# A decoder layer on one core: the recurrence's preparation in steps between projection pieces, in a written TensorE order

## The chip, the cores and the metric

One core of one Trainium2 chip runs the whole layer in one launch. The metric is the device time of an execution in microseconds; of several runs the median is given. The core has TensorE (PE; its weight loads are listed apart as PEld), VectorE (DVE), ScalarE (ACT), GpSimd (POOL) and SyncE (SP, which here only issues DMAs). Matmul results land in eight PSUM banks of 128 x 512 fp32; everything else lies in SBUF.

## The reference, cut to what matters

One layer on x of 1024 tokens by 1024 channels: a row norm, one wide projection, three branches, gates, an output projection and a convolutional FFN.

```
h = rms_norm(x, norm1_g)
proj = h @ w_in
p_rwkv, p_sb, q_mem, gate_logits = split(proj)
y_a = rwkv7_branch(p_rwkv)           # delta-rule recurrence, 8 heads x 64
y_b = stick_breaking_branch(p_sb)    # causal attention, 8 heads x 64
y_m = memory_branch(q_mem, mem)      # cross attention into 256 tokens
merged = sum_n sigmoid(gates[n]) * (ys[n] @ w_branch[n])
x = x + merged @ w_out
x = x + conv_ffn(rms_norm(x), ...)
```

In the recurrence r, k and v are mixed with the token before (token shift); a decay, a rate a and a gate g come from small low-rank products; per step S = S * w + (S @ -kk) (kk * a) + v k, y = S r, with kk the normalised k. The kernel computes it in chunks of 64 tokens.

## The kernel before

The channels lie on the partitions. Each fp32 product of a projection is made of three products of split values (hi x hi, hi x lo, lo x hi: `mm3`, line 83), so one projection of 128 channels is 8 k-blocks of six matmuls into two PSUM banks of the tag "mm". Its weights are loaded by SyncE (`load_w`, line 74), rounded by ScalarE (line 80) and the rest taken by GpSimd (line 81); two buffers each. Of the eight banks four have the tag "mm" and four the tag "g" (small products and transposes).

The stages in order:

- `startup` (line 169) loads and splits x, sums the squares of its rows (line 194), runs the first three projections k by k, and only then makes the row norm: eight products with a column of ones, a power on GpSimd (line 167), eight ScalarE copies that spread the result (line 218), transposes, and `rbc`, the norm as a full tile. All evictions of projections need `rbc` (`shifted`, lines 236 to 240).
- For each of four pairs of heads p, `rwkv_prep` (line 283) turns k, r and v into the operands of the recurrence: low-rank products and sigmoids, the sum of squares per head, a scan of the decay (line 334), exponentials, the spread of the head norm (`expand_heads`, line 246), then in two halves VectorE's chain of lines 349 to 353 and the Gram products, masked on VectorE (line 368) and written to DRAM; `turned` products of k by the decay (line 356 on GpSimd, transposes, line 383 on ScalarE). Meanwhile `rwkv_proj` runs the next pair's three projections, and after the last pair `sb_v` the value projection of the attention. `weave` (line 1503) takes some steps of one generator and then some of another; here 0.3 projection per step of the preparation.
- At this stage the order on all engines, TensorE's too, is the planner's: it sorts instructions by priority (`weave` raises that of the preparation) and by its own estimate of when operands are ready. From the attention on `self.pin` is set: matmuls and transposes then keep the order of the program (`pinned`, line 107), while the other engines' orders remain the planner's.
- `sb_attn` (line 674) is the stick-breaking attention: 64 units of head and block; `front` scores and sigmoids, a backwards scan and a multiply on VectorE (lines 698, 699), `mid` transposes, `back` the product with v. Between its steps a pump (`pumped`) takes pieces from a list of items: key and query projections (`sb_qk`), gates (`gate_item`, line 594), the memory branch's projections, later the branch products. `need(name)` pumps until a mark is set.
- `inverse` (line 388) solves the 128 triangular 64 x 64 systems of the recurrence on VectorE: 62 columns, each a product into `it` (line 395) and an addition into `inst` (line 397), on a matrix that GpSimd's queue loads from DRAM (line 386). The pump takes three of its steps per five pieces. Its results go out on GpSimd's queue (line 404) and are read by the recurrence, `stage2`, after the memory attention.
- A gate's banks are read by VectorE, which multiplies by `rbc` (line 603), followed by ScalarE's sigmoid (line 604) and a store.

The rest (branches, output projection, FFN) is not touched.

Of the kernel before, what the change touches and what calls it, by code (L numbers as in the profile page):

```python
# [14 lines left out]
AF = mybir.ActivationFunctionType  # L15
# [34 lines left out]
class Trunk:  # L50
# [118 lines left out]
    def startup(self):  # L169
# [33 lines left out]
        for k in range(8):  # L203
            ks = slice(k * 128, (k + 1) * 128)
            for w, pp in zip(ws, pps):
                self.mm3(pp, [a[:, ks] for a in w], self.xin(k), k == 0, k == 7)
        pst = self.ps("g")
        for j in range(8):
            self.mmul(pst[:, j : j + 1], sqs[-1][:, j * 128 : (j + 1) * 128], self.ones[:, 0:1], start=True, stop=True)
# [6 lines left out]
        ex = self.t4("at")  # L216
        for j in range(8):
            nc.scalar.activation(ex[:, j * 128 : (j + 1) * 128], self.ones, AF.Copy, scale=self.rsc[:, j : j + 1])
        for h in range(2):
            pt = self.ps("g")  # L220
            for j in range(4):
                self.transpose(pt[:, j * 128 : (j + 1) * 128], ex[:, (h * 4 + j) * 128 : (h * 4 + j + 1) * 128])
            nc.scalar.activation(self.rbc[:, h * 512 : (h + 1) * 512], pt, AF.Copy)
        self.wa = self.shifted(12, "A", pps[0])
        nc.scalar.activation(self.wa[0:64], self.wa[0:64], AF.Tanh)
        self.sg = self.shifted(13, "A", pps[1])
        nc.scalar.activation(self.sg, self.sg, AF.Sigmoid)
        return self.shifted(4, "at", pps[2])
# [48 lines left out]
    def rwkv_proj(self, p, out):  # L277
        for i in range(len(out), 3):
            out.append(self.shifted((4, 0, 8)[i] + p, tag="at"))
            yield  # L280

    def rwkv_prep(self, p, krv):
        nc = self.nc
        k, r, v = krv
# [3 lines left out]
        a, g = self.t4("qk"), self.t4("qk")  # L288
# [4 lines left out]
        for hs in halves:  # L293
            pgh = self.ps("g")
            self.mmul(pgh, lora[:, 512 + p * 128 : 512 + (p + 1) * 128], self.sg[:, hs], start=True, stop=True)
            nc.scalar.activation(g[:, hs], pgh, AF.Copy)
# [3 lines left out]
        yield  # L300
        su, P = self.t4("qk"), self.t4("qk", n=1025)
# [4 lines left out]
        nc.scalar.activation(P[:, :1024], k, AF.Square, scale=self.par("k_k", p))  # L306
# [5 lines left out]
        yield  # L312
# [8 lines left out]
        for cc in range(2):  # L321
            nc.scalar.dma_start(self.vd[p // 2, :, :, p % 2 * 2 + cc].rearrange("g s i -> s g i"), vt[cc * 64 : cc * 64 + 64].rearrange("s (g i) -> s g i", g=NG))
# [8 lines left out]
        nc.scalar.dma_start(self.ggd[p, 0], g)  # L331
        yield
        cc = Q = su
        nc.vector.tensor_tensor_scan(cc, self.seg, su, 0.0, ALU.mult, ALU.add)
        nc.scalar.activation(P[:, 1:1025], cc, AF.Exp, scale=-EXPM, bias=self.offs[:, 0:1])
        pc = self.pc[p]
        nc.scalar.activation(pc, cc.rearrange("p (c s) -> p c s", c=NC)[:, :, 63], AF.Exp, scale=-EXPM)
        nc.scalar.activation(Q, cc, AF.Exp, scale=EXPM, bias=self.offs[:, 1:2])
        nc.vector.memset(P[:, 0:1], 0.0)
        bc = self.bcast_heads(self.expand_heads(inv, "qk"))  # L340
        kk, b = k, a
        for h, hs in enumerate(halves):
            nc.vector.scalar_tensor_tensor(kk[:, hs], k[:, hs], self.par("k_k", p), bc[h], ALU.mult, ALU.mult)
        nc.vector.tensor_tensor(b, kk, a, ALU.mult)
        yield
        for h, hs in enumerate(halves):
            bk, ra = self.t4("qk"), self.t4("qk")
            bk4, ra4 = (x.rearrange("p (c u s) -> p c u s", c=8, u=2) for x in (bk, ra))
            nc.vector.tensor_tensor(bk4[:, :, 0], self.c8(b[:, hs]), self.c8(Q[:, hs]), ALU.mult)
            nc.vector.tensor_tensor(bk4[:, :, 1], self.c8(kp[:, hs]), self.c8(Q[:, hs]), ALU.mult)  # L350
            nc.vector.tensor_tensor(ra4[:, :, 0], self.c8(r[:, hs]), self.c8(P[:, 1 + h * 512 : 1 + (h + 1) * 512]), ALU.mult)
            nc.vector.scalar_tensor_tensor(ra4[:, :, 1], self.c8(P[:, hs]), -1.0, self.c8(kk[:, hs]), ALU.mult, ALU.mult)
            nc.vector.tensor_scalar(ra4[:, :, 1, 0], self.c8(kk[:, hs])[:, :, 0], -math.exp(OFF), None, ALU.mult)
            self.spill(p, h, 0, ra, nc.sync)
            bp = self.t4("qk")
            nc.gpsimd.tensor_tensor(
                self.c8(bp), self.c8(bk), pc[:, h * 8 : h * 8 + 8].unsqueeze(2).to_broadcast([128, 8, 128]), ALU.mult)
            for f in range(2):
                mt = self.t4("qk")
                mt4 = mt.rearrange("p (c h t) -> p c h t", c=4, h=2)  # L360
                pm = [self.ps("g"), self.ps("g")]
                for c in range(4):
                    o = (f * 4 + c) * 128
                    for h2 in range(2):
                        q = slice(h2 * 64, h2 * 64 + 64)
                        self.mmul(pm[h2][:, c * 128 : (c + 1) * 128], bk[q, o : o + 128], ra[q, o : o + 128], start=True, stop=True)
                for h2 in range(2):
                    nc.vector.tensor_tensor(
                        mt4[:, :, h2], pm[h2].rearrange("p (c t) -> p c t", c=4),
                        self.mm_mask.unsqueeze(1).to_broadcast([128, 4, 128]), ALU.mult)  # L370
                g0 = h * 4 + f * 2
                nc.sync.dma_start(
                    self.scr[p, g0 : g0 + 2, :, 512:1024].rearrange("g q c -> q g c"), mt.rearrange("q (g c) -> q g c", g=2))
                for h2 in range(2):
                    i0 = p * 32 + h2 * 16 + h * 8 + f * 4
                    nc.sync.dma_start(self.mad[i0 : i0 + 4].rearrange("c s t -> s c t"), mt4[0:64, :, h2, 64:128])
                yield
            bt = self.t4("qk")
            for f in range(2):
                pt = self.ps("g")  # L380
                for c in range(4):
                    self.transpose(pt[:, c * 128 : (c + 1) * 128], bp[:, (f * 4 + c) * 128 : (f * 4 + c + 1) * 128])
                nc.scalar.activation(bt[:, f * 512 : (f + 1) * 512], pt, AF.Copy)
            self.spill(p, h, 256, bt, nc.scalar)
            yield
        nc.gpsimd.dma_start(self.inst[p * 32 : p * 32 + 32], self.mad[p * 32 : p * 32 + 32])

    def inverse(self):
        nc = self.nc
        X = self.inst  # L390
        for s in range(1, 63):
            n = 63 - s
# [1272 lines left out]
```

## Time and profile before

| what | value |
|---|---|
| three runs | 2019.86, 2024.20, 2024.33 us, median 2024.2 |
| profiled execution | 2021.44 us, span from first to last instruction 2019.6 us |
| busy | TensorE 95%, weight loads 77%, VectorE 60%, ScalarE 43%, GpSimd 39% |
| mean granted TensorE clock | 0.978 |
| HBM traffic | 175.83 MB read, 77.33 MB written |

The profile is of one execution. An instruction of the trace has its line, engine, operation and tiles (written out<-in); "idle before" is the time in which its engine did nothing ahead of it, and the name behind the arrow is what released it. A helper's line stands for all its callers, so matmuls carry line 112 and transposes line 105. Matmuls overlap in the pipeline: their rate is read from the distance of their starts. The granted clock is 1 at the full rate; it is given as a mean over a stretch.

### The profile page before, as it was taken

What the parts mean: (1) busy time and instruction counts of PE and PEld (TensorE: products, weight loads), DVE (VectorE), ACT (ScalarE), POOL (GpSimd) and SP (SyncE); (2) the same over time, 40 slices, a digit from 0 to 9 for tenths busy, and PEclk for the clock granted to TensorE, in tenths of its full rate; (3) what the DMA queues carried; (4) which work ended last, traced back from release to release, by engine and by line L of the source; (5) the groups of instructions that cost most, each with busy time, mean ns of one, the idle gap of its engine ahead of it and who ended that gap; (6) DMA issues with size and microseconds to landing.
All of it is one profiled execution on the core that took longest, in us unless ns stands there. A gap on an engine that the chain in (4) does not pass through costs nothing. (4 is left out here: it accounts for less than half of the span.)

```text
span 2019.6 us, 26436 instructions
## 1 busy us (share of the span) xinstructions
PE 1912.1 (95%) x9940; PEld 1546.2 (77%) x9940; DVE 1212.5 (60%) x1783; ACT 874.5 (43%) x1537; POOL 795.1 (39%) x444
## 2 busy tenths in 40 slices
PE   7999989787999999998999989998999999999989
PEld 6676667676888898777777867876888888878877
DVE  4555658899756632433444268247776776786483
ACT  4444322444656653541333323344444454454433
POOL 2222233312323243111132254157767677645453
PEclk9999989888999999999999999999999999999999
DMA  4144552111122332176643354222222232377474
GB/s 186 53 140 152 167 167 84 42 37 35 48 61 58 92 100 76 48 251 195 217 144 128 147 198 170 100 107 78 100 100 96 100 118 78 115 247 276 137 240 164
DMA packets 110735, 254.92 MB, mean 126 GB/s; under 512 B 19472, under 2 KB 32016, under 8 KB 110480
## 3 DMA queue, kind: packets, MB, share of 16 engines
q1 hardware_dynamic: 78736, 190.54, 28.1%
q10 hardware_dynamic: 28096, 50.08, 7.0%
q0 software_dynamic: 3776, 12.62, 2.1%
q8 instruction: 78, 1.28, 0.3%
q14 instruction: 49, 0.40, 0.1%
HBM read 175.83 MB, written 77.33 MB: 125 GB/s over the span
## 5 line engine op out<-in xcount | busy, mean ns | idle before, releaser
L81 POOL TENSOR_TENSOR wl<-wr,wh 128x1024 fp32r<-128x1024 f32 x77 | 197.6, 2567 | 534.5 <-ACT wh L80 508.1
L112 PE MATMUL mm<-xhi,wh 128*128 128x512 f32 x784 | 271.0, 424 | 20.4 <-DVE w L603 10.7
L112 PE MATMUL mm<-xlo,wh 128*128 128x512 f32 x784 | 252.1, 401 | 0.9 <-DVE xlo L181 0.9
L112 PE MATMUL mm<-xhi,wl 128*128 128x512 f32 x784 | 252.4, 401 | 0.0
L80 ACT ACTIVATE wh<-wr 128x1024 fp32r<-128x1024 f32 x77 | 81.7, 1061 | 233.9 <-PE mm L112 204.9
L112 PEld LDWEIGHTS mm<-xlo,wh 128*128 128x128 f32 x784 | 149.9, 191 | 39.9 <-issue 3.0
L112 PEld LDWEIGHTS mm<-xhi,wl 128*128 128x128 f32 x784 | 148.9, 190 | 36.9 <-issue 1.5
L112 PEld LDWEIGHTS mm<-xhi,wh 128*128 128x128 f32 x784 | 138.9, 194 | 48.9 <-DVE w L603 11.5
L698 DVE TENSOR_TENSOR_SCAN at<-at,at 128x128 f32<-128x128 f32 (+3 forms) x64 | 90.6, 1416 | 62.6 <-ACT at L697 57.2
L112 PE MATMUL mm<-dw,da 128*128 128x512 f32 x528 | 120.7, 389 | 1.8 <-DVE da L1419 1.8
L112 PE MATMUL mm<-BT,l 128*128 128x512 f32 x504 | 119.3, 392 | 0.0
L112 PE MATMUL mm<-BT,wh 128*128 128x512 f32 x352 | 111.6, 398 | 6.9 <-DVE u L1237 6.3
L1420 POOL TENSOR_TENSOR dw<-draw,dw 128x512 fp32r<-128x512 f32 x55 | 84.5, 1540 | 85.3 <-ACT dw L1418 83.9
L112 PEld LDWEIGHTS mm<-dw,da 128*128 128x128 f32 x528 | 99.0, 188 | 22.8 <-DVE da L1419 2.2
L112 PE MATMUL mm<-B,wh 128*128 128x512 f32 x352 | 110.5, 395 | 1.7 <-ACT p L1279 1.7
L112 PEld LDWEIGHTS mm<-BT,l 128*128 128x128 f32 x504 | 94.6, 188 | 21.4
L167 POOL TENSOR_TENSOR hf<-rs,half 128x16 f32<-128x16 f32 (+1 forms) x17 | 52.6, 3094 | 123.1 <-DVE rs L166 112.2
L1417 ACT ACTIVATE da<-draw 128x512 fp32r<-128x512 f32 x77 | 48.6, 632 | 120.5 <-PE g L112 48.2
L112 PE MATMUL g<-dw,da 128*128 128x512 f32 x396 | 93.6, 398 | 5.7 <-POOL dw L1420 4.3
L1419 DVE TENSOR_TENSOR da<-draw,da 128x512 fp32r<-128x512 f32 x77 | 60.9, 798 | 54.9 <-ACT da L1417 54.9
L112 PEld LDWEIGHTS g<-dw,da 128*128 128x128 f32 x396 | 76.2, 193 | 22.6 <-POOL dw L1420 4.8
L112 PE MATMUL mm<-at,A 128*128 128x128 f32 (+1 forms) x608 | 91.2, 295 | 1.1 <-DVE qk L863 1.1
(314 smaller groups left out, 4249.3 us busy)
## 6 DMA issues: line engine op xcount, KB each, us to landing
wr<-in_w_in_dram SPq DMA_DIRECT2D x50, 512.0 KB, 3.6
draw<-actd SPq DMA_DIRECT2D x77, 256.0 KB, 3.2
at<-scr SPq DMA_DIRECT2D x32, 512.0 KB, 5.6
draw<-in_w_down_dram SPq DMA_DIRECT2D x55, 256.0 KB, 4.1
scr<-qk SPq DMA_DIRECT2D x24, 512.0 KB, 3.3
wr<-in_w_up_dram SPq DMA_DIRECT2D x22, 512.0 KB, 3.4
actd<-gall ACTq DMA_DIRECT2D x44, 256.0 KB, 3.0
rw<-in_w_up_dram SPq DMA_DIRECT2D x20, 512.0 KB, 3.5
```

Source lines behind the costliest of these rows:

```text
L80: self.nc.scalar.activation(hi, raw, AF.Copy)
L81: self.nc.gpsimd.tensor_tensor(lo, raw, hi.bitcast(F32), ALU.subtract)
L112: self.pinned(self.nc.tensor.matmul(*a, **k))
L167: nc.gpsimd.tensor_tensor(out, t[:, :n], self.half[:, :n], ALU.pow)
L698: nc.vector.tensor_tensor_scan(sn[:, :W][:, ::-1], sn[:, :W][:, ::-1], sp[:, :W], 1.0, ALU.mult, ALU.bypass)
L1417: nc.scalar.activation(A[:, 0], a, AF.Copy)
L1419: nc.vector.tensor_tensor(A[:, 1], a, A[:, 0].bitcast(F32), ALU.subtract)
L1420: nc.gpsimd.tensor_tensor(Wt[:, 1], w, Wt[:, 0].bitcast(F32), ALU.subtract)
```

## The change

- The row norm is a function of its own (`row_norm`, `row_spread`) called inside the first projections' loop, after k = 4 and after k = 6.
- `shift_item` makes a projection of r, k or v an item of the pump's list: one piece of six matmuls per step. `sb_v` becomes eight items of four pieces. Marks say when k and v of a pair are evicted (`settle`).
- `rwkv_prep` is cut into 25 steps (31 for the first pair) and rearranged: decay and scan early, the chain of lines 349 to 353 as `chain(h)`, Gram products as four separate pieces `gram(h, f)`, each a set number of steps behind the chain. Some tiles move to other buffers (`mt` and `bt` from "qk" to "at", `bp` and `ex` to "it").
- `self.pin` is set before the preparation, so TensorE's order is the program's from there on.
- The inverse takes 8 steps per ten pieces after the last preparation and 5 per ten from the attention on; what is left is drained before the branch items. Its VectorE steps, and the attention's scan and multiply (now `weigh`, half a unit later), keep the order of the program.
- A gate's banks are copied by ScalarE; VectorE then multiplies the SBUF copy.

```diff
             for w, pp in zip(ws, pps):
                 self.mm3(pp, [a[:, ks] for a in w], self.xin(k), k == 0, k == 7)
+            if k == 4:
+                self.row_norm(sqs[-1])
+            elif k == 6:
+                self.row_spread()
...
+    def shift_item(self, ti, out, name):
+        w = self.split_w(self.I["w_in"][ti])
+        yield
+        pp = [self.ps("mm"), self.ps("mm")]
+        for k in range(8):
+            ks = slice(k * 128, (k + 1) * 128)
+            self.mm3(pp, [a[:, ks] for a in w], self.xin(k), k == 0, k == 7)
+            if k == 3:
+                self.settle()
+            if k < 7:
+                yield
+        out.append(self.shifted(ti, "at", pp))
+        self.fresh.append(name)
+        yield
...
     def inverse(self):
...
-            nc.vector.tensor_tensor(tv, X[:, 0:s, s : s + 1]...
+            self.pinned(nc.vector.tensor_tensor(tv, X[:, 0:s, s : s + 1]...
...
     def gate_item, fin:
             for h in range(2):
-                hs = slice(h * 512, (h + 1) * 512)
-                nc.vector.tensor_tensor(g[:, hs], pp[h], self.rbc[:, hs], ALU.mult)
+                nc.scalar.activation(g[:, h * 512 : (h + 1) * 512], pp[h], AF.Copy)
+            nc.vector.tensor_tensor(g, g, self.rbc, ALU.mult)
             nc.scalar.activation(g, g, AF.Sigmoid)
...
+        def weigh(u):
+            W = (units[u][3] + 1) * 128
+            sn, sp = st[u]
+            self.pinned(nc.vector.tensor_tensor_scan(sn[:, :W][:, ::-1], ...))
+            self.pinned(nc.vector.tensor_tensor(sp[:, : W - 1], sp[:, : W - 1], sn[:, 1:W], ALU.mult))
...
             if 2 <= u < len(units) + 2:
                 mid(u - 2)
+            if u < len(units):
+                weigh(u)
             yield
...
-        drain(self.rwkv_proj(0, krv[0]))
-        for p in range(4):
-            f = self.rwkv_proj(p + 1, krv[p + 1]) if p < 3 else self.sb_v()
-            self.weave(self.rwkv_prep(p, krv[p]), f, 0.3)
-            drain(f)
+        self.pin = True
+        marks, self.fresh = {"k0"}, []
+        self.marks = marks
+        items = [self.shift_item(i + p, krv[p], f"{n}{p}") for p in range(4) for n, i in (("k", 4), ("r", 0), ("v", 8)) if (p, n) != (0, "k")]
+        items += self.sb_v()
+        inv = self.inverse()
...
-        items += [ld1, gate(), mark("y1"), *br1, ld2, gate(), *br2]
+        items += [lambda: drain(inv), ld1, gate(), mark("y1"), *br1, ld2, gate(), *br2]
...
-        inv = self.inverse()
+        pace = [0]
 
         def pumped():
-            for i, _ in enumerate(self.stream(items)):
-                for _ in range((i * 3 + 3) // 5 - i * 3 // 5):
+            due = 0
+            for _ in self.stream(items):
+                due += pace[0]
+                while due >= 10:
+                    due -= 10
                     next(inv, None)
                 yield
...
-        self.pin = True
+        for p in range(4):
+            self.weave(self.rwkv_prep(p, krv[p], need), pump, 1.0)
+        pace[0] = 8
+        need("sb0")
+        pace[0] = 5
         self.weave(self.sb_attn(qk, need), pump, 1.03, 0)
         need("kv")
-        drain(inv)
         self.weave(self.mem_attn(mq, need), pump, 1.6, 0)
```

The steps of the new `rwkv_prep`, with the number of pieces behind each (for p = 0 six pieces go ahead):

```
a = sigmoid(low-rank), square of k, kp            2
su = sigmoid(low-rank), scan                      2
head sums, norm, g, exponentials, spread ex       3
(needs v) rk, transposes of v, store              2
transposes of ex, kk, b; chain(0); decayed(0)     2
bonus products, stores of bonus and g             3
gram(0,0); chain(1)                               1
gram(0,1)                                         2
turned(0), decayed(1)                             3
gram(1,0)                                         1
gram(1,1)                                         3
turned(1), load of the inverse's matrix           1
```

## The prediction from the page and the trace of before

> **What bounds the kernel now.** I read the page first. TensorE is busy in nearly all of the span; the rest is what can be won.
>
> ```profile
> span 2019.6 us, 26436 instructions
> PE 1912.1 (95%) x9940; PEld 1546.2 (77%) x9940; DVE 1212.5 (60%) x1783; ACT 874.5 (43%) x1537; POOL 795.1 (39%) x444
> ```
>
> Next I cut the span by stage in the view of windows. Columns: stretch, length, then busy us and count of TensorE, weight loads, VectorE, ScalarE, GpSimd; then the granted TensorE clock, DMA share, GB/s. The rows are startup, row norm, preparation of the recurrence with its projections, the rest of those projections, the first attention inputs, early attention, later attention, everything after.
>
> ```profile
> 0.00:46.30 46.30, 38.15 (x160) 30.56 (x160) 22.89 (x23) 22.41 (x22) 11.30 (x9) 1.00 0.47 181
> 46.30:58.50 12.20, 8.37 (x24) 6.01 (x24) 5.92 (x12) 7.23 (x14) 2.73 (x2) 0.58 0.23 83
> 58.50:310.00 251.50, 231.54 (x1171) 174.59 (x1170) 139.58 (x166) 94.77 (x113) 73.11 (x32) 0.97 0.46 141
> 310.00:350.50 40.50, 40.50 (x185) 33.05 (x184) 38.15 (x40) 11.15 (x13) 13.91 (x5) 1.00 0.23 75
> 350.50:386.00 35.50, 22.34 (x100) 18.32 (x99) 27.51 (x33) 10.73 (x12) 10.17 (x3) 0.81 0.08 31
> 386.00:515.00 129.00, 110.28 (x609) 91.72 (x609) 120.58 (x133) 64.30 (x115) 26.59 (x10) 0.92 0.12 38
> 515.00:740.00 225.00, 224.99 (x1365) 192.10 (x1364) 134.76 (x144) 144.19 (x258) 67.22 (x41) 0.99 0.23 68
> 740.00:2019.60 1279.60, 1235.94 (x6339) 999.89 (x6337) 723.11 (x1236) 519.75 (x993) 590.04 (x344) 0.99 0.42 145
> ```
>
> The edits lie in the stages before 740. TensorE idles there 3.8 us in the row norm, 20.0 in the preparation, 13.2 and 18.7 at the start of attention; nothing between 515 and 740. In the same four rows the clock is low as well, so gaps cost twice. VectorE explains the shape: 120.6 of 129 us busy in early attention, 134.8 of 225 later, because the inverse, whose steps were spread over all of attention in the program, ran early.
>
> The waits of TensorE in the first 600 us (engine and what it did, releaser, us in total, times, longest) name the causes:
>
> ```profile
> PE g L112 <- DVE qk L353: 17.7, 8, 3.7
> PE g L105 <- DVE w L246: 13.2, 1, 13.2
> PE mm L112 <- DVE w L603: 10.7, 2, 8.9
> ...
> PE g L105 <- DVE at L699: 4.9, 3, 2.4
> PE g L105 <- ACT at L218: 3.1, 1, 3.1
> PE mm L112 <- ACT w L649: 1.7, 1, 1.7
> ...
> PE g L105 <- DVE hn L557: 1.4, 1, 1.4
> ```
>
> L353 is the last operand before the Gram products of the preparation; L246 spreads the head norm; L603 is VectorE taking a gate out of its banks; L699 weighs the attention; L218 belongs to the row norm.
>
> **Startup.** The row norm moves from behind the projections to the places after their fifth and seventh k. These are rows of the timeline (start, us, engine, line, operation):
>
> ```profile
> 28.82 1.21 DVE L194 TENSOR_TENSOR qk<-qk,qk 128x1024 f32<-128x1024 f32 x1
> 32.01 0.63 PE L112 MATMUL mm<-xhi,wh 128*128 128x512 f32 x2
> 40.38 0.63 PE L112 MATMUL mm<-xhi,wh 128*128 128x512 f32 x2
> 44.57 1.84 PE L112 MATMUL g<-kon,qk 128*128 128x1 f32 x16
> 49.52 2.52 PE L105 MATMUL g<-kon,at 128*128 128x128 f32 x8 [3.10 <-ACT at L218]
> 52.77 0.80 PE L112 MATMUL mm<-xhi,wh 128*128 128x512 f32 x1 [0.73 <-DVE w L236]
> 55.50 1.05 PE L112 MATMUL mm<-xhi,wh 128*128 128x512 f32 x2
> 56.35 1.05 PE L112 MATMUL mm<-xlo,wh 128*128 128x512 f32 x2
> 58.65 0.40 PE L112 MATMUL mm<-xlo,wh 128*128 128x512 f32 x1
> 77.09 0.63 PE L112 MATMUL mm<-xhi,wh 128*128 128x512 f32 x2
> 78.49 0.63 PE L112 MATMUL mm<-xhi,wh 128*128 128x512 f32 x2
> ```
>
> The last sum of squares is ready at 30.0, before the fifth k ends at 32.0; the chain from the sums to the transposes takes 49.5 - 44.6 = 5.0 us, and 8.4 lie between the two new places. So both waits of this chain (3.83) go. The matmuls themselves stay, at the full rate. After the gap a pair of matmuls takes 0.85 us (55.50 to 56.35), at the full rate 1.40 / 3 = 0.47 (77.09 to 78.49 is three pairs): from 52.77 to 58.65 that loses 5.88 x (1 - 0.47 / 0.85) = 2.6. The gain lies between 3.8, the idle alone, and 8.9, with all of the clock loss 0.42 x 12.2 = 5.1. I take 7: both waits, the 2.6 and a little of the slow transposes.
>
> **Preparation.** The same products, projections and DMAs are issued, but TensorE's order is now written: 11 projections and 8 value items give 120 pieces of six matmuls (1.40 us, above), and a preparation is cut into 25 steps with a piece after each. What can be won is all idle and clock of that row: 20.0 + 0.03 x 251.5 = 27.5. What is late next is VectorE's chain again, now with a fixed cover:
>
> ```profile
> 90.87 1.88 PE L112 MATMUL g<-qk,kon 128*128 128x512 f32 x4
> 93.40 1.39 DVE L343 SCALAR_TENSOR_TENSOR at<-at,params,g 128x512 f32<-128x512 f32 x2
> 99.57 1.75 DVE L353 TENSOR_SCALAR qk<-at 128x8 f32<-128x8 f32 x1
> 101.37 2.06 PE L112 MATMUL g<-qk,qk 64*128 64x128 f32 x32 [1.22 <-DVE qk L353]
> 112.36 3.29 PE L112 MATMUL g<-qk,qk 64*128 64x128 f32 x32 [2.51 <-DVE qk L353]
> 114.03 1.29 DVE L240 SCALAR_TENSOR_TENSOR at<-w,omm,w 128x1024 f32<-128x1024 f32 x1 [1.21 <-ACT w L238]
> ```
>
> From the first product with the spread norm (93.40) to the end of L353 (101.32) are 7.9 us. In the new order five pieces (7.0) and the bonus products (1.88) stand between the spread and the first Gram piece: 8.9. That is 1.0 to spare. If a projection's eviction falls in between (two multiplies and L240, some 2.6 us), the operand is 1.6 late. Counting steps, a projection ends inside this stretch for the first three preparations and not for the fourth. The second half has six pieces and a Gram piece, 9.4, against a chain of similar length and the mask multiplies. So I leave three to six waits of 1.6, about 7, and 2 for the clock behind them: 9 of the 27.5 stay, between 0 and 27.5. Gain 18.5.
>
> The clock needs a choice here. After the wait of 1.22 us the Gram products took 2.06, after one of 2.51 they took 3.29, so 2.51 us was enough for slow matmuls. The Trainium skill, "TensorE: Matmul & The Clock Gate", section "What's actually happening", says that the half rate comes after an idle window of about 3.4 us; by that rule my short waits would cost no clock and the forecast would be 2 us lower. The trace decides against it.
>
> Buffers moved from one tag to another are no longer waited for, by my count of live tiles; a spill or weight load that comes late has a projection's whole length of cover (eight pieces, 11 us).
>
> **The inverse and early attention.** The inverse starts after the last preparation, and its first step waits on VectorE for its matrix from DRAM, as today:
>
> ```profile
> 311.01 0.23 DVE L395 TENSOR_TENSOR it<-inst 128x62 f32<-128x62 f32 x1 [17.50 <-DMA inst<-mad]
> ```
>
> Behind it on VectorE stands the first attention head's norm, which TensorE needs after 7 + 8 + 8 pieces, 32 us: the 17.5 stay hidden; uncovered they would cost up to that. Then 0.8 steps per piece, from attention on 0.5, all pinned between the weighings. VectorE's work up to 740 stays (120.6 + 134.8 us from 386 on), over 354 - 32 = 322 us: 79% busy rather than 93% and then 60%. So the 13.2 at L246 and the 10.7 at L603 go: the norm no longer queues behind inverse steps, and gates leave through ScalarE. Idle of both rows: 31.9. The clock there: 0.19 x 35.5 + 0.08 x 129 = 17.1, but much of it falls into the gaps themselves, where it costs nothing. I take 7, 2.6 after each of three long waits as at startup. Of the 39 the waits behind the weighing and the head norm (4.9 + 1.4) and a little clock stay: 7. Gain 32, between 0 and 49.
>
> The inverse ends later, some 20 pieces (28 us) before the memory attention is through; its results then go out from GpSimd's queue before the recurrence loads them:
>
> ```profile
> L404 POOL DMA_DIRECT2D td<-inst x16 | 13.1, 821 | 29.3 <-PE g L112 29.3
> ```
>
> 13.1 us in 28: free. Without that cover the recurrence would start up to 13 late.
>
> **Gates.** Of sixteen gates each gets two ScalarE copies, and VectorE's two multiplies become one of SBUF operands, off the banks' path. ScalarE is busy half of early attention. TensorE waited for such a copy (L649) once, 1.7 us, with eight key and query evictions in attention: 0.2 each, for sixteen gates 3, between 0 and 27. It counts as a loss.
>
> **The sum.** 7 + 18.5 + 32 - 3 = 54.5. The profiled execution took 2021.4 us, 1.8 more than its span: 1967. The median of the three runs (2024.2; 2019.9 to 2024.3) is 2.8 above it; the range takes that in. About 0.3%, 6 us, can be told from no change.
>
> **Rivals.** (1) VectorE stays the bound of early attention: pinned inverse steps hold back weighings and head norms. For it: 93% busy there, and equal inverse steps differ threefold:
>
> ```profile
> 339.27 0.94 DVE L397 TENSOR_TENSOR inst<-inst,it 128x752 f32<-128x752 f32 x1
> 480.17 2.96 DVE L397 TENSOR_TENSOR inst<-inst,it 128x752 f32<-128x752 f32 x1
> ```
>
> Against it: half a step per piece is what the later row shows to be room for. Then the 32 and the gates' 3 drop out: gain 25.5, 1996. The Trainium skill, "SBUF — State Buffer", section "SBUF: two separate sides", has VectorE with two SBUF inputs and GpSimd lock each other out; the two rows fit that, and the gates' multiply joins such instructions, which speaks against the change.
>
> (2) The preparation keeps its 27.5 in other places, since its chain of VectorE steps is no shorter: gain 36, 1985.
>
> (3) Slower: the fixed order lets TensorE wait where before another projection filled in. If each of the sixteen Gram pieces waits as long as today's longest (3.7) with today's clock loss per wait (7.5 / 8 = 0.9), the preparation loses 74 instead of 27.5; with the other gains the sum is 46.5 - 36 = 10.5 slower, 2032. It decides from 4 us per Gram piece on. Against it: the pieces were counted above to cover the chain to within 2.
>
> (4) It doesn't do what it says: only TensorE, inverse and weighing are pinned, so the planner may again put VectorE's steps badly; only the startup remains, 2014, or no change.
>
> **Chances.** Forecast 0.62, its own range 1946 to 1982 (low end: 8.9 + 27.5 + 39 won in full); (1) 0.14, (2) 0.12, (3) 0.07, (4) 0.05. A range of 1946 to 2002 leaves out (3), (4) and little more. Faster 0.89, same 0.04, slower 0.07.
>
> **What would show it.** In the new profile: the transposes of the row norm before 42 us; no wait of 3 us or more on L353's successor; no wait for the head norm spread above 3 us; gates waited for on ScalarE in 1 to 2 us pieces; VectorE near 80% from the first attention unit to the last; inverse steps all through attention. Idle before the end of attention should fall from 55.7 to about 18. It is wrong if Gram waits stay near 18 us in total, if the weighing's waits grow beyond 10, or if the recurrence starts late for its inverse.

## The result, and the profile after

The changed kernel took 1988.07 us (median; 1985.24 to 1991.09), the kernel before, on the same chip, 2024.26 (2019.86 to 2025.7): a ratio of 0.9825, 95% interval 0.9802 to 0.9848. It is faster by 36 us where the sum had 54.5; the range on record (1946 to 2002) holds it, the likeliest case's own (to 1982) does not. The profiled execution took 1991.09 us. Run a second time (e8 below) it took 1984.4, with a ratio of 0.9821. The experiments ran on several chips, on which the kernel before took 2019.0 to 2024.3 us by medians, so across them the ratio to the kernel before is the fairer measure. The profile of after is of the slowest of its four executions, that of e8 of the fastest.

Where the time went is seen by four milestones that both kernels have: the first and last score matmul of the stick-breaking attention, the first and last step of the recurrence, the first and last matmul of the FFN's first half. Rows of the views of single tiles (duration min/median/max in ns, first and last start):

```profile
L112 PE MATMUL g<-sbmask,identb x64: 229/230/330, 386.2 to 737.2; 128*128 128x128 bf16 x64
L469 DVE SCALAR_TENSOR_TENSOR it<-it,pc,g x120: 258/280/290, 901.6 to 1138.2; 64x64 f32<-64x64 f32 x120
L112 PE MATMUL mm<-BT,wh x352: 387/394/628, 1377.2 to 1791.7; 128*128 128x512 f32 x176
```

These three were of before, with its span of 2019.6; of after, with a span of 1989.3:

```profile
L112 PE MATMUL g<-sbmask,identb x64: 229/230/234, 347.9 to 684.7; 128*128 128x128 bf16 x64
L532 DVE SCALAR_TENSOR_TENSOR it<-it,pc,g x120: 262/280/289, 864.6 to 1100.5; 64x64 f32<-64x64 f32 x120
L112 PE MATMUL mm<-BT,wh x352: 388/394/795, 1345.0 to 1762.5; 128*128 128x512 f32 x176
```

Differences give the stages, for the experiments too (us, one profiled execution each):

| kernel | to attention | attention | memory attention | recurrence | to the FFN | FFN up | down |
|---|---|---|---|---|---|---|---|
| before | 386.2 | 351.0 | 164.4 | 236.6 | 239.0 | 414.5 | 227.9 |
| after | 347.9 | 336.8 | 179.9 | 235.9 | 244.5 | 417.5 | 226.8 |
| e8, after again | 347.9 | 335.7 | 178.0 | 234.3 | 240.7 | 414.9 | 228.7 |
| e5, row norm late | 355.9 | 336.8 | 177.9 | 236.6 | 238.7 | 414.5 | 226.4 |
| e6, old preparation | 371.6 | 339.5 | 187.9 | 235.7 | 243.6 | 417.6 | 226.7 |
| e3, gates via VectorE | 342.2 | 351.4 | 171.5 | 233.8 | 240.6 | 417.6 | 228.9 |
| e4, VectorE free | 353.1 | 354.2 | 164.5 | 236.9 | 236.5 | 419.5 | 228.9 |
| e1, results by SyncE | 344.4 | 342.3 | 199.8 | 236.8 | 243.7 | 417.6 | 228.9 |
| e2, the same, paced | 347.4 | 345.7 | 186.4 | 236.1 | 240.8 | 414.9 | 228.8 |
| e7, results spread | 348.1 | 335.6 | 187.1 | 234.7 | 236.2 | 418.1 | 231.3 |
| e9, norm step first | 346.0 | 338.5 | 174.0 | 232.8 | 240.6 | 414.3 | 228.7 |
| e10, the same, pace 6 | 347.1 | 339.3 | 174.8 | 236.9 | 240.6 | 413.4 | 230.7 |
| e11, results after | 346.1 | 336.5 | 184.2 | 235.0 | 238.1 | 418.3 | 229.1 |
| e12, no inverse steps | 344.3 | 332.7 | 164.4 | 235.4 | 247.2 | 417.5 | 229.0 |

Up to the end of attention the change won 38.3 + 14.2 = 52.5 us: the forecast's 54.5, almost. Then the memory attention, for which the forecast had no term, gave 15.5 back (13.6 in e8). Of the 5.5 lost ahead of the FFN most is chance: a wait for VectorE's line 1322 took 8.1 us there and 3.5 in e8, the same kernel.

The stages of after in the view of windows, cut at like places (columns as before: TensorE, weight loads, VectorE, ScalarE, GpSimd busy, then clock, DMA share, GB/s):

```profile
0.00:48.00 48.00, 39.02 (x169) 30.83 (x170) 24.46 (x27) 26.32 (x33) 11.96 (x9) 1.00 0.46 174
48.00:310.00 262.00, 258.41 (x1310) 194.97 (x1309) 145.03 (x190) 106.03 (x127) 86.31 (x38) 1.00 0.49 149
310.00:347.90 37.90, 35.02 (x158) 28.32 (x156) 25.81 (x30) 14.25 (x16) 10.56 (x4) 0.91 0.13 42
347.90:476.90 129.00, 126.61 (x751) 106.71 (x749) 104.77 (x100) 81.82 (x149) 29.30 (x10) 1.00 0.16 51
476.90:684.70 207.80, 201.85 (x1205) 171.15 (x1206) 166.65 (x161) 133.43 (x240) 41.66 (x16) 0.98 0.18 54
684.70:864.60 179.90, 168.32 (x927) 138.53 (x927) 82.97 (x146) 82.23 (x163) 57.38 (x43) 0.96 0.44 120
```

VectorE is busy 81% and 80% of the two parts of attention, no longer 93% and then 60%: the inverse is spread. TensorE's idle time from 48 to the end of attention is 3.6 + 2.9 + 2.4 + 6.0 = 14.8 us, where 55.7 stood before. In the last row it idles 11.6 us at a clock of 0.96; the same stage of before has 1.1 us and the full clock, with 120 VectorE and 19 GpSimd instructions where after has 146 and 43:

```profile
737.20:901.60 164.40, 163.27 (x927) 134.88 (x927) 54.00 (x120) 78.00 (x155) 42.78 (x19) 1.00 0.34 120
```

So of the 15.5 us 10.4 are idle TensorE, and 5.1 are the same matmuls at a lower clock (168.32 - 163.27). The waits of TensorE in after (total, times, longest), those of startup, branches and FFN left out:

```profile
PE g L105 <- DVE at L783: 10.6, 6, 3.1
...
PE g L112 <- ACT at L999: 7.1, 1, 7.1
...
PE g L105 <- DVE at L392: 2.5, 2, 1.4
...
PE g L112 <- DMA at<-scr: 1.9, 1, 1.9
...
PE g L105 <- DVE w L252: 1.1, 1, 1.1
PE g L112 <- DVE qk L378: 1.0, 2, 0.8
...
PE mm L112 <- ACT w L681: 0.7, 1, 0.7
```

L378 is the old L353 (Gram operand, 17.7 before), L252 the old L246 (13.2), L681 the gates' copy (10.7 at the old L603), L783 the old L699 (weighing, 4.9). L392 masks the Gram products out of the banks that the next transposes take. L999, the copy of the memory attention's transposed scores, is new, and it is one wait of 7.1 us.

The row norm's products and transposes are where the change put them, with no wait ahead (timeline of after, TensorE):

```profile
32.74 1.84 PE L112 MATMUL g<-kon,qk 128*128 128x1 f32 x16
...
42.90 1.04 PE L105 MATMUL g<-kon,at 128*128 128x128 f32 x8
```

**The 7.1 us wait.** It lies at 812 in the memory attention. From the timeline of after, GpSimd (POOL), VectorE, ScalarE and TensorE:

```profile
780.15 6.43 POOL L467 DMA_DIRECT2D td<-inst  x8 [2.24 <-DVE inst L460]
...
799.44 0.17 DVE L166 TENSOR_SCALAR rs<-hn 128x8 f32<-128x8 f32 x1
...
800.08 1.71 POOL L467 DMA_DIRECT2D td<-inst  x2 [2.37 <-DMA td<-inst]
...
804.16 1.66 POOL L167 TENSOR_TENSOR hf<-rs,half 128x8 f32<-128x8 f32 x1
...
810.87 1.06 ACT L681 ACTIVATE w<-mm 128x512 f32<-128x512 f32 x2
...
811.96 2.56 DVE L682 TENSOR_TENSOR w<-w,rbc 128x1024 f32<-128x1024 f32 x1 [5.98 <-ACT w L681]
...
814.44 0.15 DVE L639 SCALAR_TENSOR_TENSOR hf<-hf,rsc 128x8 f32<-128x8 f32 x1
...
815.17 1.06 ACT L683 ACTIVATE w<-w 128x1024 f32<-128x1024 f32 x1
...
816.67 1.28 ACT L984 ACT_TABLE_LOAD   x1 [0.44 <-ACT w L683]
817.97 0.56 ACT L984 ACTIVATE at<-g,nb,hf 128x256 f32<-128x256 f32 x1
...
819.16 2.93 PE L112 MATMUL g<-A,qk 128*128 128x256 f32 x12 [7.12 <-ACT at L999]
```

Three things meet here. The inverse now ends at 780, its 16 stores hold GpSimd's queue until 801.8, a weight's split (line 81) follows, and the power of the query norm (L167), whose input is ready at 799.6, comes out at 805.8. And VectorE then stands on the gate's multiply (L682), which waits 5.98 us for ScalarE's copies, with the norm's last step (L639, 0.15 us, ready since 805.8) behind it until 814.4. Last, the exponentials (L984), whose operands are ready at 814.9, stand on ScalarE behind the gate's sigmoid (L683) and a table load (ACT_TABLE_LOAD, 1.28 us): 3.1 us more. The transposes and TensorE follow. After the wait the twelve products take 2.93 us, where the same twelve took 1.60 before it. Which of these costs the time was the question for the experiments; theory A, at first, was the row of stores, and its rival the order of VectorE. ScalarE's order was not tested by a run of its own.

### The profile page after: what moved, and what is told of

It reads as the page before. It is cut to its first block, busy times and chain, and to the rows that moved or that the text cites. A ratio compares the mean times of both kernels' runs of the same rounds, so it can differ in the third digit from the quotient of the medians.

```text
span 1989.3 us, 26460 instructions
## 1 busy us (share of the span) xinstructions
PE 1912.8 (96%) x9940; PEld 1544.9 (78%) x9940; DVE 1226.1 (62%) x1759; ACT 896.8 (45%) x1585; POOL 793.3 (40%) x444
## 3 DMA queue, kind: packets, MB, share of 16 engines
q8 instruction: 78, 1.28, 0.3%
## 5 line engine op out<-in xcount | busy, mean ns | idle before, releaser
L112 PE MATMUL mm<-xhi,wl 128*128 128x512 f32 x784 | 248.1, 398 | 0.1
L80 ACT ACTIVATE wh<-wr 128x1024 fp32r<-128x1024 f32 x77 | 81.8, 1062 | 179.3 <-PE mm L112 126.8
L112 PE MATMUL mm<-BT,wh 128*128 128x512 f32 x352 | 114.4, 407 | 11.6 <-DVE u L1322 11.6
L782 DVE TENSOR_TENSOR_SCAN at<-at,at 128x128 f32<-128x128 f32 (+3 forms) x64 | 98.2, 1535 | 23.1 <-ACT at L776 22.9
L1504 DVE TENSOR_TENSOR da<-draw,da 128x512 fp32r<-128x512 f32 x77 | 65.2, 856 | 51.3 <-ACT da L1502 51.3
L1271 POOL TENSOR_TENSOR l<-it,l 128x1024 fp32r<-128x1024 f32 x21 | 50.3, 2395 | 102.5 <-ACT l L1270 102.5
```

The source lines that it names most:

```text
L80: self.nc.scalar.activation(hi, raw, AF.Copy)
L112: self.pinned(self.nc.tensor.matmul(*a, **k))
L782: self.pinned(nc.vector.tensor_tensor_scan(sn[:, :W][:, ::-1], sn[:, :W][:, ::-1], sp[:, :W], 1.0, ALU.mult, ALU.bypass))
L1271: nc.gpsimd.tensor_tensor(lo, src, hi.bitcast(F32), ALU.subtract)
L1504: nc.vector.tensor_tensor(A[:, 1], a, A[:, 0].bitcast(F32), ALU.subtract)
```

## The experiments

### One part of the change undone

**e5, the row norm behind the first projections again.**

```diff
-            if k == 4:
-                self.row_norm(sqs[-1])
-            elif k == 6:
-                self.row_spread()
+        self.row_norm(sqs[-1])
+        self.row_spread()
```

> One part undone: the row norm goes back behind the first projections, all else as in the changed kernel. The prediction's 7 us for this part: 1994 to 1996 us, with the transposes behind 44 us, a gap of about 3 us and slow matmuls after it. If only the idle counts (3.8): 1991 to 1993. If the written order of TensorE makes it dearer, since the first preparation's steps now wait too: above 1997.

Measured: 1989.21 us (1988.53 to 1991.27), ratio 0.9844 [0.9827, 0.9862]. The wait behind the spread copies is back, 3.1 us, and the first stage is 8.0 us longer than in e8. The whole is only 1 to 5 us longer than the two medians of the changed kernel (4.8 than e8, on the same chip), so less than the stage shows and below all the times that were expected; the intervals overlap.

**e6, the preparation as it was**: `rwkv_prep`, `rwkv_proj`, the weave at 0.3 and TensorE's order left to the planner until attention; all else as changed.

> One part undone: preparation, projections of r, k, v and the value projection as before (TensorE's order the planner's until the attention), all else as in the changed kernel. The prediction's 18.5 us for this part: 2004 to 2009 us, with waits of 1.2 to 3.7 us ahead of the Gram products. If the stage is held by VectorE either way (rival 2): 1988 to 1992.

Measured: 2018.93 us (2010.01 to 2024.4), 0.9989 [0.9973, 1.0005]. Nearly all of the gain is gone; the time is 10 us above the highest that was expected. Its waits of TensorE have the Gram operand back to the digit:

```profile
PE g L112 <- DVE qk L363: 17.7, 8, 3.7
```

The first stage is 23.7 us longer than in e8, attention 3.8, memory attention 9.9. (The profiled execution is the slowest of twelve, 2024.4.) The last two are not the preparation's own: the inverse starts later behind it and is pushed further into what follows, so that its first store goes out at 837.9 instead of 780.1.

**e3, gates taken out of the banks by VectorE again.**

```diff
-                nc.scalar.activation(g[:, ...], pp[h], AF.Copy)
-            nc.vector.tensor_tensor(g, g, self.rbc, ALU.mult)
+                nc.vector.tensor_tensor(g[:, ...], pp[h], self.rbc[:, ...], ALU.mult)
```

> One part undone: VectorE again takes a gate out of its banks with the norm's multiply, no ScalarE copies. If the pacing of the inverse alone removed the waits on gates (the prediction's cost of 3 us for the copies): 1984 to 1988 us. If the copies are needed because VectorE, now busy all through attention, would hold banks: waits of 1 to 3 us on such evictions come back at several of the sixteen gates, 1993 to 2000 us.

Measured: 1987.9 us (1985.95 to 1988.32), 0.982 [0.9806, 0.9834]: no difference. The waits of TensorE change places, all the same:

```profile
PE mm L112 <- DVE w L681: 15.2, 3, 6.8
...
PE g L105 <- DVE at L782: 3.7, 3, 2.1
```

15.2 us of waits for gates come back (0.7 in after), and attention is 15.7 us longer than in e8; but the weighing's waits fall by two thirds, the first stage is 5.7 and memory attention 6.5 shorter. ScalarE's copies free the banks sooner, other waits grow with them, and the sum is nothing.

**e4, the inverse and the weighing not kept in program order** (`pinned` left out at lines 458, 460, 782 and 783).

> One part undone: the inverse's steps and the attention's scan and multiply no longer keep the program's order on VectorE; paces and TensorE's order stay. If the fixed order is what spreads the inverse (the planner ran it early before): VectorE is again over 90% busy in early attention, waits for the head norm's spread and the weighing come back, 2000 to 2015 us. If the pace in the program suffices: 1984 to 1992 us with inverse steps all through attention.

Measured: 1992.77 us (1990.15 to 1995.4), 0.9842 [0.9828, 0.9857]. The inverse runs early again (its last step at 497.5 instead of 779.6), attention takes 354.2 us, and memory attention is what it was before the change (view of windows):

```profile
707.30:871.80 164.50, 163.37 (x928) 134.91 (x928) 60.13 (x117) 82.12 (x163) 42.89 (x27) 1.00 0.36 118
```

Spreading the inverse over attention wins 18.5 us there and 5.2 ahead of it, and pays 13.5 in memory attention. The waits are those of the first expectation; the time lies between the two (above 1992 and under 2000). By medians 5 to 8 us are left to the fixed order, by ratios 3 to 4.

**e8, the changed kernel unchanged**, for the spread between runs.

> The changed kernel again, on the same chip as its variants: 1985 to 1991 us. If the 8.1 us wait in the FFN at 1345 us is part of it, it is in this profile as well; if it is chance, about the 2.7 us of before.

Measured: 1984.4 us (1981.99 to 1989.83), 0.9821 [0.98, 0.9841]. The waits of 6.5 us at L999 and 11.1 at the weighing are there again (its lines count one higher), so they belong to the kernel; the FFN's wait is 3.5 us here, so its 8.1 is not in every execution.

### What memory attention gives back

**e1, the inverse's results by SyncE instead of GpSimd**: line 467 issues on `nc.sync`.

> One edit to the changed kernel: the inverse's sixteen result stores leave GpSimd's queue for SyncE's; TensorE's order stays the same. Theory A (the late inverse gives time back in the memory attention: its stores hold GpSimd from 782.6 to 803.5 us, the power for a head norm comes late, the planner therefore puts a gate's multiply ahead of the norm's last step on VectorE, and TensorE waits 7.1 us at 819 and then runs slowly): that wait goes, with its clock 8 to 10 us, 1978 to 1980 us. Theory B (the memory attention's own chain sets its length, whatever GpSimd does): 1986 to 1990, the wait stays or moves. If the stores on SyncE hold back the recurrence's loads, a wait for them of up to 5 us appears at its start.

Measured: 2004.35 us (1999.09 to 2015.3; the profiled execution is the longest), 0.9907 [0.9884, 0.9929]: 16 to 20 us worse than the changed kernel. The 7.1 us wait is gone, but in this build VectorE has L639 ahead of L682, so that is no proof of the stores' part. The loads behind the stores came late; a row of SyncE's timeline:

```profile
798.58 51.97 SPq L467 DMA_DIRECT2D td<-inst  x12
```

12 stores held SyncE's queue 52 us, 4.3 each, and the recurrence waited for its own input, which the expectation had not reckoned with at this size (waits of TensorE):

```profile
PE g L112 <- DMA qk<-vd: 22.2, 2, 19.7
```

**e2, the same with a denser pace** (12 steps per ten pieces ahead of attention, 6 in it), so that the stores lie earlier, at 668 to 704.

> As the run before, and the inverse runs faster: 12 steps per ten pieces ahead of the attention instead of 8, then 6 instead of 5, so that it ends before the short pieces of the memory branch's keys and values, where GpSimd splits weights almost without a pause. Theory A: the waits behind the weighing at 691 and 699 us (3.3 us and slow matmuls after) go too, 3 to 5 us below the run before. Theory B, VectorE is full in early attention: the waits only move forward, the weighing's total of 10.6 us grows, and the time is the same as the run before or up to 6 us more.

Measured: 2004.13 us (2001.32 to 2006.87), 0.9902 [0.9887, 0.9917]. Now the weights of a projection stand behind them; its waits of TensorE:

```profile
PE mm L112 <- ACT wh L80: 18.1, 1, 18.1
PE g L105 <- DVE at L783: 12.1, 4, 7.9
```

The same price at another place: at both places where the 16 stores went on SyncE's queue, a wait of 18 to 20 us of TensorE came with them. GpSimd's queue is the better place. The weighing's waits in memory attention are gone, but one of 7.9 us stands earlier, and the time is that of e1: theory B, as far as the stores let it be seen.

**e7, the stores on GpSimd one per piece**, with a `yield` behind each and pace 10 from the memory attention on.

> The changed kernel with the inverse's sixteen result stores issued one per piece, still on GpSimd's queue, and ten steps of the inverse per ten pieces during the memory attention, so that they are out in time. Theory A (the stores in one row on GpSimd delay the head norm's power, and TensorE waits 7.1 us for it): the wait at 819 us goes without a new one at the recurrence's start, 1978 to 1982 us. Theory B (that wait is the planner's chance, not the row of stores): 1986 to 1990, a wait of this size stays somewhere in the memory attention.

Measured: 1995.48 us (1991.56 to 1998.56), 0.9871 [0.9852, 0.9889]; memory attention 187.1. The stores ended at 797.5, before the norm's sums were there at all; they cannot hold anything up. The wait stayed at 6.8 us, and its timeline of VectorE shows why:

```profile
806.10 0.17 DVE L166 TENSOR_SCALAR rs<-hn 128x8 f32<-128x8 f32 x1
...
818.63 2.84 DVE L683 TENSOR_TENSOR w<-w,rbc 128x1024 f32<-128x1024 f32 x1 [5.99 <-ACT w L682]
821.39 0.15 DVE L640 SCALAR_TENSOR_TENSOR hf<-hf,rsc 128x8 f32<-128x8 f32 x1
```

The gate's multiply stands ahead of the norm's step here too (both lines count one higher). The stage's two other waits for ScalarE's results, 3.0 us at 772 and 2.3 at 799, have the same form: the norm's step comes at 770.3 and 795.5, 11 and 13 us after its power, behind an eviction (L949) that waits for ScalarE. So theory A, the row of stores, falls as the cause of this wait, though the time is above what either theory expected. The order on VectorE, A' below, was formed from this run.

**e9, the head norm's last step and the gate's multiply kept in program order.** Nothing else.

```diff
-        nc.vector.scalar_tensor_tensor(v3(f), v3(f), fold, b3(self.rsc), ...)
+        self.pinned(nc.vector.scalar_tensor_tensor(v3(f), v3(f), fold, b3(self.rsc), ...))
...
-            nc.vector.tensor_tensor(g, g, self.rbc, ALU.mult)
+            self.pinned(nc.vector.tensor_tensor(g, g, self.rbc, ALU.mult))
```

> The changed kernel with one thing more: VectorE keeps the program's order between the head norm's last step (L639) and the gate's multiply (L682), which in the changed kernel stands ahead of it in memory attention. Theory A' (the 6.5 to 7.1 us TensorE wait before the norm-fed matmuls of memory attention comes from VectorE's order, the multiply waiting for ScalarE's copies while the norm step is ready 8.6 us earlier): the wait falls under 1 us, memory attention goes from 178.0 to 168-171, and the time from 1984-1988 to 1975-1981. Theory B (the wait is what is left of GpSimd's late stores and of a lower granted clock): the wait stays or another of the same size takes its place, 178 stays, 1984-1988.

Measured: 1978.22 us (1976.83 to 1981.02), 0.979 [0.9773, 0.9808]; its interval just overlaps those of the changed kernel, and every one of its five runs is below all four of e8, on another chip. Rows of its timeline, VectorE, ScalarE and TensorE:

```profile
805.85 0.16 DVE L639 SCALAR_TENSOR_TENSOR hf<-hf,rsc 128x8 f32<-128x8 f32 x1
...
809.86 1.06 ACT L80 ACTIVATE wh<-wr 128x1024 fp32r<-128x1024 f32 x1 [6.06 <-PE mm L112]
...
813.10 0.56 ACT L984 ACTIVATE at<-g,nb,hf 128x256 f32<-128x256 f32 x1 [0.46 <-ACT ys L1009]
...
814.29 1.87 PE L112 MATMUL g<-A,qk 128*128 128x256 f32 x12 [2.29 <-ACT at L999]
815.96 1.05 PE L112 MATMUL mm<-xhi,wh 128*128 128x512 f32 x2
816.82 1.05 PE L112 MATMUL mm<-xlo,wh 128*128 128x512 f32 x2
...
817.66 1.22 DVE L682 TENSOR_TENSOR w<-w,rbc 128x1024 f32<-128x1024 f32 x1
```

The norm's step comes 8.6 us earlier, the wait is 2.3 instead of 6.5 to 7.1, and memory attention 174.0. The time was in the expected bounds, the stage was not: 168 to 171 had been expected. What stays above the 164.4 of before is the wait of 2.3 us, the weighing's waits of 3.4 at the stage's start, and 3.9 of matmuls at a lower clock. The 2.3 are ScalarE's order: the exponentials' operands are ready at 806.3 (VectorE's L981), but a weight's copy (L80) that waits 6.06 us for TensorE stands ahead of them, and they start at 813.1. This version has the lowest time of those that compute the whole layer.

**e10, e9 with pace 6 in attention.** The counter gives steps per ten pieces, so 6 is denser than 5; the expectation has the direction the wrong way round, and its second outcome speaks of a sparser pace, which was not tried.

> As norm_first, with one step of the inverse for every 6 units of the pace's counter in attention where the changed kernel has 5. If the inverse's steps are what VectorE cannot fit beside attention (pace too dense), weighing's waits (10.6 to 11.1 us in 6) fall by 3 us or more and more of the inverse goes to memory attention: the sum is the same as norm_first within 4 us. If its late end is what costs memory attention, the sparser pace lengthens that stage by another 3 to 8 us beside norm_first, and the time is longer by as much.

Measured: 1982.61 us (1980.5 to 1984.62), 0.981 [0.9792, 0.9827]: 4.4 us above e9 by medians, with intervals that overlap. The weighing's waits are 8.9 in all, as in e9 (9.0). The inverse ended at 734, the stores lay at 734 to 753, and VectorE's load in memory attention fell from 84.1 to 75.0 us. The stage stayed (174.8), since the wait at L999 went and another came, for a weight's split that stood on GpSimd behind the last stores and a norm's power (757.8; the row is of memory attention alone):

```profile
PE mm L112 <- POOL wl L81: 3.5, 1, 3.5
```

The split's operand was ready at 752.6 and it began at 755.4: so where the stores meet GpSimd's other work they can cost something, up to 2.8 us here, the power's 1.7 included. At the place of the 7.1 us wait the exponentials start, at 812.9, as soon as their operand is there.

**e11, the 16 stores and their loads behind the last projection of memory attention.**

> The changed kernel with the inverse's 16 stores, and their loads back, moved behind the last projection of memory attention; nothing else. If the stores on GpSimd's queue hold up memory attention (the norm's operand is made on GpSimd behind them): its 6.5 to 7.1 us wait goes, and the stage falls to 168-172; but the first loads of the recurrence then come after the stores (16 at 1.7 to 4.0 us of issue each), so a wait of 0 to 20 us stands before the first steps: 1975 to 2000. If the wait is VectorE's order alone, it stays within 2 us with the stores gone, and the time is 1984 or more.

Measured: 1987.3 us (1985.51 to 1989.1), 0.9833 [0.9815, 0.9851]. The 7 us wait is gone; but VectorE has the norm's step first in this build too (803.8 against 809.3 for the multiply), so the run does not separate the two causes. In its place, within that stage:

```profile
PE g L112 <- DVE ys L520: 4.4, 1, 4.4
...
PE mm L112 <- ACT ys L1016: 2.9, 1, 2.9
```

and the stage is 184.2 us, longest of those with GpSimd's stores but e6's and e7's. The stores must go out before the loads of the recurrence and not after.

**e12, the changed kernel without the inverse's 124 VectorE steps**; it leaves the solution of the triangular systems out.

> The changed kernel without the 124 VectorE steps of the inverse (left out: the solution of the triangular systems; the places of the program where they stood, the matrix's load, and the 16 stores and their place stay). It measures what the inverse costs where the change put it. If its steps on VectorE are the whole cost: memory attention goes from 178.0 to 164-166 with no wait above 1.5 us, the weighing's 11.1 us of waits fall to 0-2, attention goes from 335.7 to 325-332, and the time from 1984-1988 to 1957-1967, which is what the forecast of 1967 took for granted. If VectorE's order of the gate's multiply and the head norm costs memory attention without the inverse too: the wait of 6.5 us or one over 4 us stays there and the time is 1968-1980.

Measured: 1965.1 us (1962.44 to 1972.24), 0.9731 [0.9707, 0.9756]; its profiled execution, the longest of six, took 1972.24 and has the 8.1 us wait in the FFN. The stores did not stay where they were: with nothing ahead of them the planner issued them from 291 to 497. Memory attention is that of before (view of windows):

```profile
677.00:841.40 164.40, 163.27 (x927) 134.82 (x927) 62.90 (x117) 82.00 (x163) 41.72 (x19) 1.00 0.35 119
```

The weighing's waits fall from 11.1 to 4.0, attention to 332.7. Here the planner puts the norm's step first by itself (788.3 against 798.9). So the inverse, its steps and its late stores together, costs 19 to 23 us by medians (18 to 19 by ratios) where the change put it, 13.6 to 15.5 of them in memory attention. The first outcome that was expected came true, but for the weighing's waits, of which 0 to 2 had been expected to stay, and 0.7 us of attention.

## Why the prediction was off by 21 us

**Right:** the direction, the terms up to the end of attention (52.5 to 53.6 against 54.5), and the signs that were named for them: Gram waits 1.0 us in all, head norm 1.1, gates 0.7, VectorE at 80%, idle 14.8 against about 18. The transposes of the row norm start at 42.9, not before 42; nothing hung on that.

**The terms inside that sum were sized less well.** Startup: 7 forecast, 8.0 in its stage (e5), within the bounds. Preparation: 18.5 forecast, 23.7 in its stage (e6). I left 9 us there for Gram waits of 1.6 us and their clock; TensorE idles 3.6 us in the whole stage, the Gram waits are 1.0 and the clock is 1.00. The written order covers the chain better than my count of pieces said. Inverse and early attention: 32 less 3 for the gates forecast, 52.5 - 8.0 - 23.7 = 20.8 found, by subtraction, in e8 21.9. The gates' loss of 3 was not seen: by e3 the copies win between nothing and 3.5 us. The waits of 4.9 and 1.4 that I had left standing became 7.3 within attention, all of it weighing. That the sum came out is luck: 1.0 and 5.2 us too little and some 8 too much nearly cancel.

**The step that failed** is the one on the inverse's results: "13.1 us in 28: free. Without that cover the recurrence would start up to 13 late." I looked for the price at the recurrence. That was not late: its longest wait for a load is 1.9 us, and its first step comes 85 us after the inverse's end. The size was too small as well: in one row the stores held GpSimd for 21.6 us, 8.7 of which it waited for earlier ones to land. The price is in between, in memory attention, 13.6 to 15.5 us. The late inverse took VectorE's and GpSimd's time there; the query norm, made of small steps on these two engines in turn, fell behind a gate's multiply on VectorE, and TensorE waited for it. e9 shows that this order costs 4 to 6 us of the stage and 6 to 10 of the time by medians (6 to 7 by ratios); e12 and e4 show that the whole of the rest goes when the inverse is not there, or is done earlier. Of the rest, 9.6 us in e9, the weighing's 3.4 lie some 80 us ahead of the first store, so the steps and not the stores cost them; 2.3 are ScalarE's order, and 3.9 the clock. Whether the late stores made the planner choose these orders is open: each run that moved the stores also moved VectorE's order or the pace (e1, e7, e10, e11). The clock is the smaller part: 5.1 of 15.5 us in after.

A second sign was named and came out: "if the weighing's waits grow beyond 10". They are 10.6 and 11.1. I had put VectorE as the bound of early attention in rival (1), with 1996. It is not the bound there (TensorE idles 2.4 of the first 129 us), but the same mechanism acts later, from 676 on, where GpSimd's splits of weights for short projections lie close together, five in 22 us. From the timeline of after, VectorE and GpSimd at the end of attention:

```profile
690.43 2.75 POOL L81 TENSOR_TENSOR wl<-wr,wh 128x1024 fp32r<-128x1024 f32 x1 [3.34 <-ACT wh L80]
...
690.87 3.02 DVE L458 TENSOR_TENSOR it<-inst 128x650 f32<-128x650 f32 x1
...
694.58 3.64 POOL L81 TENSOR_TENSOR wl<-wr,wh 128x1024 fp32r<-128x1024 f32 x1 [1.40 <-ACT wh L80]
...
696.19 3.12 DVE L783 TENSOR_TENSOR at<-at,at 128x1023 f32<-128x1023 f32 x1
...
699.23 0.82 DVE L460 TENSOR_TENSOR inst<-inst,it 128x650 f32<-128x650 f32 x1
```

The inverse's product of 650 elements takes 3.02 us beside a split, its addition of as many 0.82 without one; the multiply of 1023 takes 3.12 beside one, 1.2 without (1.21 at 609.9), and TensorE waits 3.1 us for it. The Trainium skill, "SBUF — State Buffer", section "SBUF: two separate sides", says that GpSimd and a VectorE instruction with two SBUF inputs hold a shared port by turns, each for a whole instruction; these rows agree, since both VectorE instructions end 0.7 to 1.1 us after the split beside them. Of the weighing's 10.6 us, 3.3 are paid in this place.

**The other rivals.** (2), that the preparation keeps its 27.5, would have given 1985, close to what was measured, and is wrong all the same: 23.7 of them are won. A time that fits says little for a mechanism. (3) is wrong, the Gram waits went; (4) is wrong in its price, the waits named by the change all went. But what (4) feared, a VectorE order that the planner chooses badly, is what happened in memory attention, with 7.1 us of wait, at instructions that the change left free.

## What to carry to other kernels

Work that is moved off a crowded stage is paid for in the stage that it is moved into: ask of the new place, as of the old, which short chains run over the same engines there, and what the planner will put ahead of them. Fix the order of the short, early steps (a norm's last step of 0.15 us) when the order of the long ones is fixed, and never leave a short step that TensorE waits for behind one that waits for another engine, on ScalarE no less than on VectorE. To judge a change of several parts, cut both traces at common milestones first: a stage that nothing was meant to touch is where the missing gain lies.

## What the runs showed of the hardware

- A store of one of the 16 results took SyncE's queue 4.3 us in e1 and 2.2 in e2 (35.7 for 16), and GpSimd's 1.4 (780.2 to 801.8 for 16). In one row on GpSimd they took 11.9 us from issue to landing in the median; in the kernel before, spread from 511.7 to 699.4, 4.7. One after the other on SyncE they held TensorE up by 18 to 20 us.
- TensorE's clock fell after waits of 7.1, 3.1 and, in e9, 2.3 us: in e9 pairs of matmuls then start 0.85 us apart, and 0.47 later. In e10 the slow pairs set in 1.1 us after a wait of 3.5 us had ended, and lasted 3 us. The Trainium skill, "TensorE: Matmul & The Clock Gate", section "What's actually happening", speaks of an idle window of about 3.4 us; the measured 2.3 decides against it here, as the trace of before did with 2.5.
